# Gated linear attention steps ahead of the selections in a background queue (transformer block, one core)

## The chip, the cores and the metric

One core of a Trainium2 chip runs the whole block as one program. The metric is device time in microseconds (us), the median of several executions. Engines are named as the profile names them: PE (TensorE), DVE (VectorE), ACT (ScalarE), POOL (GpSimd) and SP (SyncE, which issues most transfers).

## What is computed

One layer for a sequence of 1024 positions and width 1024. The part that the change touches is this (cut from the reference):

```python
# attention over the 256 best keys of each query, by an indexer's score
s_idx = einsum('bthd,bsd->bths', q_idx, k_idx)
score = where(causal, einsum('bths,bth->bts', relu(s_idx), w_idx * idx_scale), -inf)
_, sel = lax.top_k(score, 256)
...
# gated linear attention, chunk by chunk
b = cumsum(gc)
A = einsum('bhid,bhjd,bhijd->bhij', qc, kc, exp(b_i - b_j))     # lower triangle
o = einsum('bhij,bhjv->bhiv', A, vc) + einsum('bhid,bhdv->bhiv', qc * exp(b), S)
S = exp(b_last) * S + einsum('bhjd,bhjv->bhdv', kc * exp(b_last - b), vc)
...
x = x + g1 * (concat([rms(att), rms(gla) * silu(go)]) @ w_out)
x = x + g2 * ((silu(gate) * up) @ w_down)
```

## The kernel before

The kernel splits 32-bit operands into a high and a low part and takes three products of them. Its first 160 us or so make the normalised input, the indexer's projections and the scores. The last third and more is the feed-forward part, and ahead of it stands attention (from about 506 us on). Between scores and attention, from 147 to 506 us, stands the stretch of this change: a **main** line of projections on PE, and a **background** of work that is woven into it.

**The main line** is `units(jobs, gq0)`: a list of jobs, each a weight group and a generator. `proj_T_plain` (and `qk_proj`, `qk_park`) yields twice a job, after chains of 24 matmuls of 512 columns (`chain_T`, L241 to L243); below this is a T chain, and such a step says `LONG` = 1.87. `proj_N_plain` yields eight times a job, after chains of 24 matmuls of 256 columns (`chain_N`, L250 to L252); below this is an N chain, a step of 1. `gate_proj` ends with eight steps of `SHORT` = 0.3, without a matmul, which do L911 on DVE. The jobs are, in order: gq0, gk0, gv0, park 2q, gq1, gk1, park 2k, gv1, go0, park 3q, v0, park 3k, v1, go1, and the queries and keys of heads 0 and 1. The weights of the next job are loaded and split when a job begins: the low part is L218 (DVE or POOL).

**The background** is the table `bg`. After each main step, `pump(steps)` goes through it: an entry's `due` grows by its rate times the step's weight, and for each whole unit one step of its generator is issued. The entries are

- `ta` and `td`, the selections. They find the 256th largest score of each row bit by bit, 32 steps each. A step of `ta` is three Sign activations with sums on ACT (L647) and then four little operations on DVE (L649 to L654), each of 128x3 elements. A step of `td` is three compares with sums on DVE (L617) and two little operations (L621, L623). Then each has three steps that call `finish`, which turns a threshold into the mask tile `bias[t]` (L593 to L601);
- `gla0` and `gla1`, the gated linear attention of two pairs of heads (`gla_pair`). For seven levels there are `decays` (POOL L784 and L785, ACT L786), `decayed` (DVE L793, POOL L798), `products` (PE L804) and `masked` (DVE L813), each a step behind the one before. Then come transposes (PE L851, copied by ACT L852), and eight chunks: a DVE operation makes the carried state `diag` (L881, L883), the PE multiplies (L865, L868, L872), the DVE puts the output together (L893);
- `decay`, which prepares the second pair.

The order in `bg` is that of insertion, so `ta` and `td` come first. `pin()` then ties the PE and DVE instructions of the stretch to the order in which they were written: on these two engines the schedule is the program's text. ACT, POOL and SP are ordered by the framework's scheduler. `gs` tiles are a pool of four buffers, `raw` (weights as loaded) of two, `whi` and `wlo` of four.

Of the kernel before, what the change touches and what calls it, by code (L numbers as in the profile page):

```python
# [8 lines left out]
F32 = mybir.dt.float32  # L9
# [8 lines left out]
P = 128  # L18
L = 1024
# [20 lines left out]
WO_POOL = (1, 3, 5, 7)  # L40
H_ACT, H_POOL = (0, 4, 7), (0, 1, 3, 4, 6)

RATE = {"ta": (0.46, 0), "td": (0.46, 1), "gla0": (0.67, 0), "gla1": (0.6, 0), "decay": (0.5, 0),
        "mod2": (1.5, 0), "mods": (1.2, 0), "side": (0.42, 0.6)}

LONG, SHORT = 1.87, 0.3
PRIORITY = {"side": 150, "mods": -40}

PARK_AT = (3, 6, 9, 11)

# [16 lines left out]
def hymba_block_kernel(  # L67
# [44 lines left out]
    def gs(shape, dt=F32):  # L112
        return g(shape, dt, tag="gs", bufs=NGS)
# [234 lines left out]
    bg = {}  # L348

    def pump(steps=1):  # L350

        for name in list(bg):
            it, rate, due = bg[name]
            due += rate * steps
            while due >= 1:
                due -= 1
                with tc.high_priority(PRIORITY[name]) if name in PRIORITY else nullcontext():
                    end = next(it, "end") == "end"
                if end:
                    del bg[name]  # L360
                    break
            else:
                bg[name] = (it, rate, due)

    def drain(name):
# [18 lines left out]
    def gv_proj(p, w):  # L384
        drain("decay")
        gvt[p] = [g([P, 4, 256]) for _ in range(2)]
        if p == 0:
            bg["gla0"] = (gla_pair(0, gqk[0, 0], gqk[0, 1], gvt[0], bTs[0]), *RATE["gla0"])
        yield from proj_N_plain(w, gvt[p])
        if p == 0:  # L390
            bg["decay"] = (gla_decay(1), *RATE["decay"])
        else:
            drain("gla0")
            bg["gla1"] = (gla_pair(1, gqk[1, 0], gqk[1, 1], gvt[1], bTs[1]), *RATE["gla1"])

# [152 lines left out]
    def scores(t):  # L548
        W = (t + 1) * P
        acc = score[t]  # L550
# [34 lines left out]
        return -1.0 if i == 0 else float(1 << (31 - i))  # L585

    def finish(t, thr):
        W = (t + 1) * P
        xs = score[t]
        two = gs([P, 2 * L], BF16)  # L590
        lt, eq = two[:, :W], two[:, L:L + W]
        n2 = small(2, tag="n1")
        V.tensor_scalar(lt, xs, thr, None, ALU.is_lt, ALU.add, accum_out=n2[:, 0:1])  # L593
        V.tensor_scalar(eq, xs, thr, None, ALU.is_equal, ALU.add, accum_out=n2[:, 1:2])
        run = gs([P, L])
        V.tensor_tensor(n2[:, 0:1], n2[:, 0:1], n2[:, 1:2], ALU.add)
        V.tensor_scalar(n2[:, 0:1], n2[:, 0:1], float(TOPK - W), None, ALU.add)
        V.tensor_tensor_scan(run[:, :W], eq, eq, 0.0, ALU.add, ALU.max)
        V.scalar_tensor_tensor(eq, run[:, :W], n2[:, 0:1], eq, ALU.is_gt, ALU.mult)
        V.tensor_tensor(lt, lt, eq, ALU.add)  # L600
        V.tensor_scalar(bias[t], lt, -OFF_BIAS, None, ALU.mult)  # L601

    def topk_dve(ts):
        n = len(ts)
        Z = cst.tile([P, n], I32, name="Zd")
        V.memset(Z, 0)
        for t in ts:
            hi = score[t].bitcast(BF16)[:, 1:2 * (t + 1) * P:2]
            if t in TOP_POOL:
                G.tensor_scalar(top[t], hi, 1.0, 0.0, ALU.mult, ALU.add)  # L610
            else:
                V.tensor_copy(top[t], hi)
        for i in range(32):
            acc = small(8, tag="acc")
            for j, t in enumerate(ts):
                W = (t + 1) * P
                V.tensor_scalar(junk_d[:, :W], top[t] if 0 < i < 16 else score[t],  # L617
                                Z[:, j:j + 1].bitcast(F32), -float(TOPK),
                                ALU.is_ge, ALU.add, accum_out=acc[:, j:j + 1])
            m = small(8, I32, tag="md")  # L620
            V.tensor_scalar(m[:, :n], acc[:, :n], 0.0, flip(i), ALU.is_lt, ALU.mult)  # L621
            if i < 31:
                V.scalar_tensor_tensor(Z, m[:, :n], nextbit(i), Z, ALU.bitwise_xor, ALU.bitwise_xor)  # L623
            else:
                V.tensor_tensor(Z, m[:, :n], Z, ALU.bitwise_xor)
            yield
        bias_tiles((5, 4, 3))
        for j, t in enumerate(ts):
            finish(t, Z[:, j:j + 1].bitcast(F32))
            yield  # L630

    def topk_act(ts):
        n = len(ts)
        Y = cst.tile([P, n], I32, name="Ya")
        F = cst.tile([P, n], I32, name="Fa")
        need = cst.tile([P, n], F32, name="need")
        V.memset(Y.bitcast(F32), 0.0)
        V.tensor_scalar(Y, Y, -2147483648, None, ALU.bitwise_xor)
        V.tensor_copy(F.bitcast(F32), Y.bitcast(F32))
        for j, t in enumerate(ts):  # L640
            V.memset(need[:, j:j + 1], float(2 * TOPK - (t + 1) * P))
        for i in range(32):
            acc = small(8, tag="acca")
            m = small(8, I32, tag="ma")
            for j, t in enumerate(ts):
                W = (t + 1) * P
                A.activation(junk_a[:, :W], score[t], AF.Sign, bias=Y[:, j:j + 1].bitcast(F32),  # L647
                             accum_out=acc[:, j:j + 1])
            V.tensor_tensor(acc[:, :n], acc[:, :n], need, ALU.subtract)  # L649
            V.tensor_scalar(m[:, :n], acc[:, :n].bitcast(I32), 31, -1 if i == 0 else 1 << (31 - i),  # L650
                            ALU.arith_shift_right, ALU.bitwise_and)
            V.copy_predicated(F, m[:, :n], Y)
            if i < 31:
                V.scalar_tensor_tensor(Y, m[:, :n], nextbit(i), Y, ALU.bitwise_xor, ALU.bitwise_xor)  # L654
            else:
                V.tensor_tensor(Y, m[:, :n], Y, ALU.bitwise_xor)
            yield
        bias_tiles((7, 6))
        V.tensor_scalar(Y, Y, -2147483648, None, ALU.bitwise_xor)
        V.tensor_scalar(F, F, -2147483648, None, ALU.bitwise_xor)  # L660
        for j, t in enumerate(ts):
            W = (t + 1) * P
            a1 = small(1, tag="a1")
            V.tensor_scalar(junk_a[:, :W], score[t], F[:, j:j + 1].bitcast(F32), -float(TOPK),
                            ALU.is_ge, ALU.add, accum_out=a1)
            m = small(1, I32, tag="m1")
            V.tensor_scalar(m, a1, 0.0, None, ALU.is_ge)
            V.copy_predicated(Y[:, j:j + 1], m, F[:, j:j + 1])
            finish(t, Y[:, j:j + 1].bitcast(F32))
            yield  # L670


    sh2 = cst.tile([P, KC], F32, name="sh2")
# [93 lines left out]
    def gla_pair(p, gq, gk, gv, bT):  # L767
# [83 lines left out]
            T.transpose(pt[:, cc * P:(cc + 1) * P], gk[:, cc * P:(cc + 1) * P], ident)  # L851
        A.copy(bT, pt)  # L852
        Kn = bT.rearrange("p (a b) -> p a b", b=P)
        yield
        o = gv
        gla_o[p] = o
# [105 lines left out]
    for t in range(4, 8):  # L962
        scores(t)
    bg["ta"] = (topk_act(SEL_A), *RATE["ta"])
    bg["td"] = (topk_dve(SEL_D), *RATE["td"])
    before, mark = {}, [len(nc.cur_bb.bb.instructions)]

# [571 lines left out]
```

## Time and profile before

| | |
|---|---|
| median of 3 runs | 1425.96 us (1423.41 to 1428.74) |
| the profiled execution | 1424.55 us, span 1422.7 us |
| PE busy | 1323.1 us (93%) |
| DVE busy | 913.9 us (64%) |
| ACT busy | 585.5 us (41%) |
| POOL busy | 446.7 us (31%) |
| chain that ended last | PE 63%, DVE 19%, issue 6%, DMA 4%, ACT 4%, POOL 3% |
| granted PE clock, mean | 0.97 |

The shares are means over the whole program. The feed-forward part keeps PE at 10 tenths almost throughout, so the places where PE waits have to be looked for by stretch. A row of a timeline gives the start, the duration, the engine and line, and in brackets the idle time of that engine before it and what ended the idle time.

### The profile page before, as it was taken

The page shows a single profiled execution, that of the slowest core. Times are in us where ns is not written, and L with a number is a line of the kernel's source. Part 1 is how long each engine was busy: PE and PEld are TensorE (multiplying, and loading weights), DVE is VectorE, ACT ScalarE, POOL GpSimd, SP SyncE. Part 2 cuts the span into 40 slices and gives each one's busy share as a digit, 9 for nine tenths or more (in the row PEclk, how much of TensorE's full clock was granted, in tenths as well). Part 3 has the DMA queues.
Part 4 walks back from the last instruction along what each step waited for, and adds up shares of the span by engine and source line. Part 5 has one row for each costly group of instructions (what it writes and reads, how often), then busy time and mean ns, then how long its engine had stood idle before and what let it go on. Part 6 is the DMA issues. An engine that isn't in the chain of part 4 may idle for free.

```text
span 1422.7 us, 18374 instructions
## 1 busy us (share of the span) xinstructions
PE 1323.1 (93%) x6979; PEld 1107.5 (78%) x6979; DVE 913.9 (64%) x1525; ACT 585.5 (41%) x1064; POOL 446.7 (31%) x393
## 2 busy tenths in 40 slices
PE   5899978699899889899997999999999999999997
PEld 4777877498789768788886887778888878888886
DVE  3579889848976935776468656655454556566524
ACT  3377654557464235345574333232233335112202
POOL 3560524413300011223322444334444425232101
PEclk9999989799899999999998999999999999999999
DMA  9600110200220235551221343322212346254102
GB/s 271 201 15 1 32 43 15 60 31 31 90 60 17 71 107 177 208 192 60 86 93 45 104 134 118 104 89 75 88 64 86 108 152 216 94 186 148 45 15 104
DMA packets 93630, 136.35 MB, mean 96 GB/s; under 512 B 6404, under 2 KB 72039, under 8 KB 93543
## 3 DMA queue, kind: packets, MB, share of 16 engines
q1 hardware_dynamic: 89576, 121.49, 26.6%
q0 software_dynamic: 3808, 13.64, 3.0%
q8 instruction: 55, 0.90, 0.3%
q14 instruction: 33, 0.26, 0.1%
q10 hardware_dynamic: 158, 0.06, 0.0%
HBM read 111.04 MB, written 24.13 MB: 95 GB/s over the span
## 4 chain that ended last, share of the span: by engine, by line
PE 63%; DVE 19%; issue 6%; DMA 4%; ACT 4%; POOL 3%; SPq 2%; POOLq 0%; ACTq 0%; DVEq 0%
PE pw L1273 4%; PE pw L1274 4%; PE pw L1275 4%; PE ps L1273 4%; PE ps L1275 4%; PE ps L1274 4%; PE ps L1480 3%; PE ps L1479 3%; PE ps L1481 3%; PE pw L1480 3%; PE pw L1481 2%; PE pw L1479 2%; DVE junk_d L617 2%; DVE h L793 2%; PE ps L250 2%
## 5 line engine op out<-in xcount | busy, mean ns | idle before, releaser
L647 ACT ACTIVATE junk_a<-g,Ya 128x1024 int8<-128x1024 f32 (+2 forms) x96 | 99.9, 1040 | 53.7 <-DVE Ya L654 50.6
L250 PE MATMUL ps<-whi,g 128*128 128x256 f32 x384 | 111.6, 291 | 0.2 <-ACT g L345 0.2
L251 PE MATMUL ps<-whi,g 128*128 128x256 f32 x384 | 109.4, 285 | 0.0
L252 PE MATMUL ps<-wlo,g 128*128 128x256 f32 x384 | 109.3, 285 | 0.0
L1304 POOL TENSOR_TENSOR g<-g,h 128x512 f32<-128x512 f32 x33 | 52.3, 1584 | 139.8 <-issue 53.4
L1445 POOL TENSOR_TENSOR raw<-raw,g 128x1024 f32<-128x1024 f32 x22 | 57.5, 2618 | 111.8 <-DMA raw<-in_w_down_dram 103.3
L243 PE MATMUL ps<-g,wlo 128*128 128x512 f32 x208 | 83.1, 400 | 4.8 <-DVE wlo L218 4.8
L241 PE MATMUL ps<-g,whi 128*128 128x512 f32 x208 | 85.3, 410 | 0.0
L242 PE MATMUL ps<-g,whi 128*128 128x512 f32 x208 | 83.1, 399 | 0.0
L1275 PE MATMUL ps<-g,wlo 128*128 128x512 f32 x192 | 76.0, 396 | 6.3 <-DVE wlo L1266 6.2
L1273 PE MATMUL pw<-g,whi 128*128 128x512 f32 x192 | 76.9, 400 | 1.5 <-DVE h L1322 1.5
L1273 PE MATMUL ps<-g,wlo 128*128 128x512 f32 x192 | 76.0, 396 | 0.7 <-ACT g L1178 0.7
L250 PEld LDWEIGHTS ps<-whi,g 128*128 128x128 f32 x384 | 74.6, 194 | 2.6 <-issue 1.7
L1274 PE MATMUL ps<-g,wlo 128*128 128x512 f32 x192 | 75.7, 394 | 0.4 <-DVE g L1179 0.4
L1274 PE MATMUL pw<-g,whi 128*128 128x512 f32 x192 | 74.9, 390 | 0.0
L1275 PE MATMUL pw<-g,whi 128*128 128x512 f32 x192 | 74.7, 389 | 0.0
L251 PEld LDWEIGHTS ps<-whi,g 128*128 128x128 f32 x384 | 74.5, 194 | 0.0
L252 PEld LDWEIGHTS ps<-wlo,g 128*128 128x128 f32 x384 | 74.4, 194 | 0.0
L617 DVE TENSOR_SCALAR_CACHE_REDUCE junk_d<-g,Zd 128x640 bf16<-128x640 f32 (+5 forms) x96 | 71.4, 743 | 2.3
L1242 POOL TENSOR_TENSOR gs<-raw,raw 128x512 f32<-128x512 f32 x19 | 25.4, 1334 | 119.2 <-DMA raw<-in_w_gate_up_dram 119.2
L1266 DVE TENSOR_TENSOR wlo<-gs,wlo 128x512 fp32r<-128x512 f32 x44 | 39.9, 906 | 29.1 <-ACT wlo L1265 28.6
L1266 DVE TENSOR_TENSOR whi<-gs,whi 128x512 fp32r<-128x512 f32 x44 | 38.7, 879 | 30.9 <-ACT whi L1265 30.4
(408 smaller groups left out, 3881.3 us busy)
## 6 DMA issues: line engine op xcount, KB each, us to landing
raw<-in_w_gate_up_dram SPq DMA_DIRECT2D x42, 512.0 KB, 3.6
g<-in_w_mod_dram SPq DMA_DIRECT2D x24, 512.0 KB, 8.1
raw<-in_w_in_dram SPq DMA_DIRECT2D x24, 512.0 KB, 3.7
whi<-in_w_mod_dram POOLq DMA_DIRECT2D x24, 512.0 KB, 4.8
hid_d<-g SPq DMA_DIRECT2D x22, 512.0 KB, 3.0
raw<-in_w_down_dram SPq DMA_DIRECT2D x22, 512.0 KB, 4.4
gs<-hid_d SPq DMA_DIRECT2D x22, 512.0 KB, 3.5
g<-in_x_dram SPq DMA_DIRECT2D x16, 512.0 KB, 4.5
```

The costliest lines, as they stand in the source:

```text
L241: T.matmul(pt, lhsT=wh, rhs=rh, start=(k == 0), stop=False)
L242: T.matmul(pt, lhsT=wh, rhs=rl, start=False, stop=False)
L243: T.matmul(pt, lhsT=wl, rhs=rh, start=False, stop=(k == KC - 1))
L250: T.matmul(pt, lhsT=rh, rhs=wh, start=(k == 0), stop=False)
L251: T.matmul(pt, lhsT=rl, rhs=wh, start=False, stop=False)
L252: T.matmul(pt, lhsT=rh, rhs=wl, start=False, stop=(k == KC - 1))
L617: V.tensor_scalar(junk_d[:, :W], top[t] if 0 < i < 16 else score[t], Z[:, j:j + 1].bitcast(F32), -float(TOPK), ALU.is_ge, ALU.add, accum_o ...
L647: A.activation(junk_a[:, :W], score[t], AF.Sign, bias=Y[:, j:j + 1].bitcast(F32), accum_out=acc[:, j:j + 1])
L1273: T.matmul(pt, lhsT=w[:, 0, kk, :], rhs=rh, start=(not more and kk == 0), stop=False, skip_group_check=more)
L1274: T.matmul(pt, lhsT=w[:, 0, kk, :], rhs=rl, start=False, stop=False, skip_group_check=more)
L1275: T.matmul(pt, lhsT=w[:, 1, kk, :], rhs=rh, start=False, stop=(kk == 3), skip_group_check=more)
L1480: T.matmul(po[m], lhsT=al[:, r], rhs=wh[:, cc], start=False, stop=False)
```

## The change

Five edits, all in the order and the pace of the background; no instruction is added or dropped.

- `pump` goes through the table with `ta` and `td` last.
- An entry of `CHAINS` (the two gated linear attentions) issues at most one step in a main step; what is due beyond that stays due.
- Rates and starting values: the selections begin with `due` = -1.5 instead of 0 and 1 and run at 0.52 instead of 0.46; the linear attentions run a little faster, and the first begins with 0.9.
- `finish` yields after the two counts, after the scan and at its end, so that a selection's end is three steps a tile; the scan's tile `run` is allocated later.
- `gla_pair` has one more empty step between the transposes' copy and the first chunk.

```diff
-RATE = {"ta": (0.46, 0), "td": (0.46, 1), "gla0": (0.67, 0), "gla1": (0.6, 0), "decay": (0.5, 0),
+RATE = {"ta": (0.52, -1.5), "td": (0.52, -1.5), "gla0": (0.69, 0.9), "gla1": (0.62, 0), "decay": (0.5, 0),
         "mod2": (1.5, 0), "mods": (1.2, 0), "side": (0.42, 0.6)}
...
+CHAINS = ("gla0", "gla1")
...
-        for name in list(bg):
+        for name in sorted(bg, key=lambda name: name in ("ta", "td")):
             it, rate, due = bg[name]
             due += rate * steps
             while due >= 1:
...
                 if end:
                     del bg[name]
                     break
-            else:
+                if name in CHAINS:
+                    break
+            if name in bg:
                 bg[name] = (it, rate, due)
...
         V.tensor_scalar(eq, xs, thr, None, ALU.is_equal, ALU.add, accum_out=n2[:, 1:2])
-        run = gs([P, L])
         V.tensor_tensor(n2[:, 0:1], n2[:, 0:1], n2[:, 1:2], ALU.add)
         V.tensor_scalar(n2[:, 0:1], n2[:, 0:1], float(TOPK - W), None, ALU.add)
+        yield
+        run = gs([P, L])
         V.tensor_tensor_scan(run[:, :W], eq, eq, 0.0, ALU.add, ALU.max)
+        yield
         V.scalar_tensor_tensor(eq, run[:, :W], n2[:, 0:1], eq, ALU.is_gt, ALU.mult)
         V.tensor_tensor(lt, lt, eq, ALU.add)
         V.tensor_scalar(bias[t], lt, -OFF_BIAS, None, ALU.mult)
+        yield
...
-            finish(t, Z[:, j:j + 1].bitcast(F32))
-            yield
+            yield from finish(t, Z[:, j:j + 1].bitcast(F32))
...
         A.copy(bT, pt)
         Kn = bT.rearrange("p (a b) -> p a b", b=P)
         yield
+        yield
```

Three places of the order follow. Rows of the changed kernel have that file's own line numbers, 2 to 7 higher: its L799 is L793, L656 to L661 are L649 to L654, L625 is L617, L872, L875 and L879 are L865, L868 and L872, L918 is L911, L220 is L218.

**DVE, up to the first `decayed`** (L793; in the changed file L799), which feeds the first `products` of the linear attention. Before, four selection steps (L649 to L623) stand ahead of it, of which the last is this, and another follows at once:

```order
L623 SCALAR_TENSOR_TENSOR Zd<-md_1595,Zd 128x3
L649 TENSOR_TENSOR acca_1686<-acca_1686,need 128x3
L650 TENSOR_SCALAR ma_1687<-acca_1686 128x3
L652 COPY_PREDICATED Fa<-ma_1687,Ya 128x3
L654 SCALAR_TENSOR_TENSOR Ya<-ma_1687,Ya 128x3
L617 TENSOR_SCALAR junk_d,acc_1695<-g_800,Zd 128x640
L621 TENSOR_SCALAR md_1699<-acc_1695 128x3
L623 SCALAR_TENSOR_TENSOR Zd<-md_1699,Zd 128x3
L793 TENSOR_TENSOR h_1130<-g_709,gs_1656 64x4x64 x2
L793 TENSOR_TENSOR h_1131<-g_709,gs_1656 64x4x64 x2
L649 TENSOR_TENSOR acca_1763<-acca_1763,need 128x3
```

After, two stand ahead of it, and the second `decayed` follows after one more:

```order
L631 SCALAR_TENSOR_TENSOR Zd<-md_1608,Zd 128x3
L799 TENSOR_TENSOR h_1130<-g_709,gs_1591 64x4x64 x2
L799 TENSOR_TENSOR h_1131<-g_709,gs_1591 64x4x64 x2
L656 TENSOR_TENSOR acca_1672<-acca_1672,need 128x3
L661 SCALAR_TENSOR_TENSOR Ya<-ma_1673,Ya 128x3
L625 TENSOR_SCALAR junk_d,acc_1681<-g_800,Zd 128x640
L631 SCALAR_TENSOR_TENSOR Zd<-md_1685,Zd 128x3
L799 TENSOR_TENSOR h_1132<-g_709,gs_1668 64x4x64 x2
L799 TENSOR_TENSOR h_1133<-g_709,gs_1668 64x4x64 x2
L656 TENSOR_TENSOR acca_1732<-acca_1732,need 128x3
```

(Of each selection step the compares of the two other tiles and some of the little operations are left out here, and in the two places below rows that add nothing.) Two selection steps have moved from ahead of the first `decayed` to behind it.

**PE, the first two chunks of the first linear attention.** Before, both stand behind the same T chain of job park 2k; the second (`pw_2342`) reads the state `diag` that DVE makes from the first (`pw_2335`):

```order
L243 MATMUL ps_2293<-g_155,wlo_2169 128x512
L865 MATMUL pw_2335<-g_1554,g_1624 128x128 x2
L872 MATMUL pw_2335<-g_1554,g_986 64x128 x2
L865 MATMUL pw_2342<-g_1554,g_1624 128x128
L868 MATMUL pw_2342<-diag_2340,g_709 128x128
L872 MATMUL pw_2342<-g_1554,g_986 64x128 x2
L241 MATMUL ps_2355<-g_696,whi_2168 128x512
```

After, the first stands behind that job's second T chain, and an N chain of job gv1 (the L252 to L254 rows, 24 in all) lies between the two:

```order
L245 MATMUL ps_2328<-g_783,wlo_2162 128x512
L872 MATMUL pw_2354<-g_1531,g_1559 128x128 x2
L879 MATMUL pw_2354<-g_1531,g_986 64x128 x2
L252 MATMUL ps_2390<-whi_2275,g_129 128x256
L253 MATMUL ps_2390<-whi_2275,g_130 128x256
L254 MATMUL ps_2390<-wlo_2276,g_129 128x256
L872 MATMUL pw_2418<-g_1531,g_1559 128x128
L875 MATMUL pw_2418<-diag_2416,g_709 128x128
L879 MATMUL pw_2418<-g_1531,g_986 64x128 x2
```

The second chunk has moved behind a T chain and an N chain. On DVE its `diag` now has thirteen selection steps ahead of it, where it had twelve of `ta`, and of `td` twelve too, the first having been done among the scores.

**DVE, the end of the selections.** Before, the last tile's mask is made (L598 to L601), then the sixteen output products of the second gate (L911), then the low part of the weights of head 0's keys (L218, `wlo_4437`):

```order
L598 SCALAR_TENSOR_TENSOR gs_4352<-gs_4348 128x768
L599 SCALAR_TENSOR_TENSOR gs_4348<-gs_4352,n_677_4349,gs_4348 128x768
L600 TENSOR_TENSOR gs_4348<-gs_4348 128x768
L601 TENSOR_SCALAR g_4091<-gs_4348 128x768
L911 SCALAR_TENSOR_TENSOR g_4128<-g_2425,rs_4413,g_4128 128x128 x8
L911 SCALAR_TENSOR_TENSOR g_4129<-g_2426,rs_4413,g_4129 128x128 x8
L218 TENSOR_TENSOR wlo_4437<-raw_4434,whi_4436 128x1024
L404 TENSOR_TENSOR g_4441<-ps_4442,g_4440 128x512
```

After, the same weights (`wlo_4431`) stand ahead of the last step of `finish`, and ten of the sixteen products ahead of its scans:

```order
L918 SCALAR_TENSOR_TENSOR g_4147<-g_2388,rs_4403,g_4147 128x128 x8
L918 SCALAR_TENSOR_TENSOR g_4148<-g_2389,rs_4403,g_4148 128x128 x2
L604 SCALAR_TENSOR_TENSOR gs_4417<-gs_4389 128x768
L604 SCALAR_TENSOR_TENSOR gs_4419<-gs_4395 128x384
L918 SCALAR_TENSOR_TENSOR g_4148<-g_2389,rs_4403,g_4148 128x128 x6
L220 TENSOR_TENSOR wlo_4431<-raw_4428,whi_4430 128x1024
L702 TENSOR_SCALAR h_4619<-whi_4569,cs 128x512
L408 TENSOR_TENSOR g_4435<-ps_4436,g_4434 128x512
L606 SCALAR_TENSOR_TENSOR gs_4389<-gs_4417,n_676_4390,gs_4389 128x768
```

The 32nd step of the selections has moved as well, from behind the last chain of job v1 to behind its second.

## Rows read from the trace of the kernel before

**Rows 1.** The page's first line.

```profile
span 1422.7 us, 18374 instructions
```

**Rows 2.** Windows: stretch, length, busy of PE, PEld, DVE, ACT, POOL, PEclk, DMA.

```profile
159.00:205.00 46.00, 36.25 (x257) 34.51 (x256) 35.21 (x92) 29.48 (x55) 17.21 (x15) 0.89 0.05 12
205.00:273.00 68.00, 48.77 (x245) 40.22 (x243) 66.12 (x117) 36.26 (x54) 29.03 (x19) 0.87 0.16 47
273.00:315.00 42.00, 41.51 (x270) 35.53 (x270) 19.84 (x72) 22.34 (x63) 4.79 (x2) 0.93 0.12 38
338.00:385.00 47.00, 37.16 (x234) 34.27 (x233) 44.67 (x87) 23.31 (x36) 21.30 (x14) 0.89 0.26 79
```

**Rows 3.** Timeline of PE: the first matmul after each long wait.

```profile
184.94 0.55 PE L804 MATMUL pw<-h,gs 128*128 128x128 f32 x1 [9.35 <-DVE h L793]
...
227.32 0.55 PE L804 MATMUL pw<-h,gs 128*128 128x128 f32 x1 [5.51 <-DVE h L793]
...
265.95 0.48 PE L872 MATMUL pw<-g,g 128*64 128x128 f32 x2 [7.88 <-ACT g L852]
...
273.49 0.55 PE L868 MATMUL pw<-diag,g 64*128 64x128 f32 x1 [6.12 <-DVE diag L881]
...
358.77 0.55 PE L804 MATMUL pw<-h,gs 128*128 128x128 f32 x1 [5.50 <-DVE h L793]
...
377.03 0.35 PE L804 MATMUL pw<-h,gs 128*128 128x128 f32 x1 [3.41 <-DVE h L793]
...
494.73 0.79 PE L243 MATMUL ps<-g,wlo 128*128 128x512 f32 x1 [4.84 <-DVE wlo L218]
...
512.83 0.69 PE L999 MATMUL pw<-g,g 128*128 128x384 f32 x1 [5.32 <-DVE mx L1004]
```

**Rows 4.** Timeline of DVE: the first selection steps, and the first state `diag`.

```profile
163.70 0.50 DVE L649 TENSOR_TENSOR acca<-acca,need 128x3 f32<-128x3 f32 x1 [4.69 <-ACT junk_a L647]
...
171.66 0.16 DVE L649 TENSOR_TENSOR acca<-acca,need 128x3 f32<-128x3 f32 x1 [1.00 <-ACT junk_a L647]
...
174.90 0.16 DVE L623 SCALAR_TENSOR_TENSOR Zd<-md,Zd 128x3 int32<-128x3 int32 x1
...
273.06 0.28 DVE L881 COPY diag<-pw 128x128 f32<-128x128 f32 x1
```

**Rows 5.** Groups of DVE from 159 to 273 us: busy, mean ns, idle before.

```profile
L654 DVE SCALAR_TENSOR_TENSOR Ya<-ma,Ya 128x3 int32<-128x3 int32 x12 | 9.0, 750 | 0.4
...
L649 DVE TENSOR_TENSOR acca<-acca,need 128x3 f32<-128x3 f32 x12 | 6.4, 533 | 9.0 <-ACT junk_a L647 8.9
```

**Rows 6.** Timeline of DVE at the end of the scores.

```profile
151.80 1.02 DVE L638 TENSOR_SCALAR Ya<-Ya 128x3 int32<-128x3 int32 x1
```

**Rows 7.** Timeline of POOL, then of DVE, at one place.

```profile
231.15 3.39 POOL L836 TENSOR_TENSOR gs<-g,g 128x1024 f32<-128x1024 f32 x1 [4.70 <-PE pw L804]
...
232.19 2.36 DVE L649 TENSOR_TENSOR acca<-acca,need 128x3 f32<-128x3 f32 x1
```

**Rows 8.** Timeline of PE: first matmuls after chunk 7, of job go1, of head 0's queries.

```profile
315.07 0.38 PE L250 MATMUL ps<-whi,g 128*128 128x256 f32 x1
...
455.23 0.38 PE L250 MATMUL ps<-whi,g 128*128 128x256 f32 x1
...
478.36 0.40 PE L241 MATMUL ps<-g,whi 128*128 128x512 f32 x1
```

**Rows 9.** Groups of DVE from 455 to 506 us: busy, mean ns, idle before.

```profile
L593 DVE TENSOR_SCALAR_CACHE_REDUCE gs<-g,Ya 128x1024 bf16<-128x1024 f32 (+2 forms) x3 | 3.4, 1146 | 0.1
```

**Rows 10.** Timelines of DVE, ACT and again DVE at the end.

```profile
489.26 4.28 DVE L911 SCALAR_TENSOR_TENSOR g<-g,rs,g 128x128 f32<-128x128 f32 x16
493.46 1.21 DVE L218 TENSOR_TENSOR wlo<-raw,whi 128x1024 fp32r<-128x1024 f32 x1
...
499.57 1.05 ACT L217 CAST whi<-raw 128x1024 fp32r<-128x1024 f32 x1 [14.95 <-DMA raw<-in_w_in_dram]
...
511.02 1.54 DVE L698 SCALAR_TENSOR_TENSOR h<-whi,cs,h 128x512 f32<-128x512 f32 x2 [4.88 <-DMA whi<-in_w_mod_dram]
```

More of the change, by code (lines that the diff above doesn't have):

```diff
@@ L668, in topk_act @@
             V.copy_predicated(Y[:, j:j + 1], m, F[:, j:j + 1])
-            finish(t, Y[:, j:j + 1].bitcast(F32))
-            yield
+            yield from finish(t, Y[:, j:j + 1].bitcast(F32))
     sh2 = cst.tile([P, KC], F32, name="sh2")
```

## The prediction

> **What bounds the kernel now.** I read the page first: span 1422.7 us [rows 1], PE busy for 93% of it. A change that only reorders can win at most what PE waits, so I next looked for its waits. The timeline of PE from 147 to 506 us holds eight of over 3 us [rows 3]. Four lie in the first linear attention: 9.35, 5.51, 7.88, 6.12 = 28.9 us. Two lie in the second: 5.50 + 3.41 = 8.9. Two lie at the end: 4.84 + 5.32 = 10.2. Together 47.9 us.
>
> Then the windows [rows 2]: who is full while PE waits? From 205 to 273 us DVE is busy for 66.12 of 68, PE for 48.77. From 273 to 315 it turns round: PE 41.51 of 42, DVE 19.84. From 338 to 385 DVE is full again, 44.67 of 47. So in these stretches the time is that of DVE's program, and PE's order matters only where it needs DVE's results.
>
> What fills DVE is in its timeline [rows 4]. From the little operations at 171.66 to the last at 174.90 (+0.16), a selection step, one of `ta` with one of `td`, takes 3.4 us, of which the little four of `ta` are 0.7. At 273.06 stands the first `diag`, for which PE waits last: DVE gets there 114 us after the scores' last operation (163.70 less 4.69 idle = 159.0). Of these 114 us DVE waits 9.0 for ACT's counts [rows 5], so 105 are work.
>
> Not all of that is its own work. The groups [rows 5] give the four little operations away: L654 takes 750 ns and L649 533 on the mean, but 0.16 alone [rows 4]. These two alone lose 15.4 - 24 x 0.16 = 11.6 us. Where it goes is seen at one place [rows 7]: L649 starts at 232.19 while POOL's L836 runs, lasts 2.36 instead of 0.16, and ends with it (234.55 and 234.54). DVE stood still for POOL.
>
> **The change, part by part.** The same instructions run, so I price only places.
>
> *First linear attention.* Three things move DVE's first `diag`.
>
> 1. The start. td's first step (2.7 us: 3.4 less 0.7) now comes after the scores; two `wlo` of about 1.2 (as one in [rows 10]) and two little operations of 1.02 [rows 6] stand ahead of the scores' products instead of among them. That is 2.7 + 2.4 + 2.0 = 7.1 us off the scores' end: DVE is done at 152, not 159.0. The bounds: 156, if PE's scores set their end, and 152.
> 2. The work. One more selection step (thirteen of each for twelve, `td`'s first among them): +3.4. Two casts of weights that now stand ahead of `diag`, for which ACT's L217 with 1.05 [rows 10] is the nearest row, `td`'s preparation of a single copy in it: +2.0 (bounds 0 and 3). So 105 + 5.4 = 110.4 us.
> 3. The idle time before L649, 9.0: as the linear attention now fills in, I take 6; bounds 0 and 9.
>
> 152 + 110.4 + 6 gives the first `diag` at 268.5 instead of 273.06. That alone is 4.6 us. The larger part is on PE: the second chunk, which reads `diag`, now stands behind one more T chain and one more N chain. From the start of the eight N chains at 455.23 to 478.36 [rows 8] one takes 2.89. From 478.36 to 489.9 (494.73 less its wait of 4.84) PE ran 50 matmuls of 512 columns, 0.23 each, so a T chain of 24 is 5.5 (at the 0.40 of the first's record, 9.6: the bound). PE, which waited 28.9 us, has time for these 8.4 us in its waits, so after `diag` it has 8.4 us less to do. Before, from 273.49 [rows 3] to the step after chunk 7 at 315.07 [rows 8] are 41.58, nearly all of it PE's work; that becomes 33.2, which ends at about 302. **-13 us.** Check from the other side: PE without a wait would have reached the old place at 273.49 - 28.9 = 244.6 and reaches the new one at 253; it waits 268.5 - 253 = 15.5 instead of 28.9, which is 13.4 less. DVE has room behind: 19.84 busy of 42.
>
> *Second linear attention.* `products` of the last level stands one N chain sooner, one selection step more stands ahead, and the rest has the same density. DVE is full here, so its work sets the time: **0**, with bounds of -8.9 (both waits go) and +3.4 (the selection step).
>
> *`finish` among the last chunks.* The counts of the first two tiles now stand between two chunks: two counts of 1.15 [rows 9] and two shorter ones, at most 4 x 1.15 = 4.6 us, beside a T chain of 5.5 on PE. I take 0; if the cover is gone, up to +4.6.
>
> *The end.* PE waits 4.84 us at 494.73 [rows 3] for `wlo` (L218), which DVE makes at 493.46, behind all three tiles' `finish` and L911 [rows 10]. Now `wlo` stands ahead of the last step of `finish`, and the selections' last step ends six steps sooner. L911 still needs the gate's last activations on ACT, after PE's N chains end at 478.36 [rows 8], so `wlo` comes at about 486, before PE wants it at 489.9 (494.73 - 4.84). **-4.8.** Behind it hangs a second chain: with `wlo` done, the buffer of `raw` is free, the next weights are loaded, ACT casts them (L217, 14.95 idle for that DMA), DVE's L698 waits for a DMA of its own, 4.88 [rows 10], and then come PE's scores of attention, with a wait of 5.32 for `mx` [rows 3]. That chain starts 7.4 us sooner (493.46 to 486), PE 4.84 sooner, so 2.6 of the 5.32 go. **-2.6.** Bounds of the two: 0 and -10.2.
>
> *DMA.* One store of queries passes one load of weights on SP's queue, two jobs before anyone reads them: 0. (DMA share in these windows: 0.05 to 0.26 [rows 2].)
>
> Sum: -13 + 0 + 0 - 4.8 - 2.6 = -20.4. The profiled execution took 1424.55 us, 1.4 below the median of 1425.96; I count from it: **1404 us**. The granted clock is 0.87 to 0.89 where PE waits [rows 2], and after the wait at 494.73 a matmul takes 0.79 at the 1.2 GHz level, where 0.40 is shown at 478.36 [rows 8]. Fewer waits may lift that; I don't count it, and let it speak for the low end.
>
> **The rivals.** What a measurement can tell from no change is about 0.5%, 7.1 us.
>
> *A. PE takes over as the bound.* If DVE, better mixed, loses none of the 11.6 us to POOL, `diag` comes at 257, only 4 after PE. The first part then gives -25 or, with ACT's idle time gone too, all 28.9; with the end's -7.4 that is 1388 to 1392. For it: the loss is a matter of meeting, not of work. Against: POOL's instructions keep their order and follow the same chains. 0.15.
>
> *B. The end doesn't move.* The last transfers may hang on something that I didn't see, and `finish` may be late all the same. Only the first part counts: 1411.5. For it: the wait before L217 is a DMA's. Against: the wait at 494.73 is DVE's, plainly. 0.14.
>
> *C. It comes back.* What PE gains in front it waits for later, since DVE's total stays: 1424. Against: the 22 us that DVE is free from 273 to 315. 0.10.
>
> *D. POOL takes the gain: slower.* POOL is busy for 17.21 + 29.03 = 46.2 us from 159 to 273 [rows 2], and DVE has lost at least 11.6 to it [rows 5, 7]. The change puts `decayed` and the masks, which follow POOL's results, ahead of the selections' little operations, so other instructions with two inputs stand beside POOL's. If all of the 46.2 were lost, that would be 34.6 more, far above the gain. It decides from 20 us more over both linear attentions (13 + 7.4). Say two thirds of POOL's time is lost: in the first 31 of 46.2, so 19 more; in the second, with POOL busy for 21.30 of 47 [rows 2] and a quarter of it lost now as in the first, 14 less 5, so 9 more. -13 + 19 + 9 - 7.4 = +7.6: 1432. For it: [rows 7]. Against: the compares of L617 are most of a selection step and keep their time. 0.09.
>
> The Trainium skill has a rule for D: on its page "SBUF — State Buffer", section "Who interferes with whom", DVE with two SBUF inputs and a GpSimd instruction that reads SBUF lock each other out for a whole instruction, and whichever starts second stands still. By that rule an order with more such pairs side by side is slower, and this one could be; the blocked L649 agrees with it.
>
> **How the numbers follow.** The forecast has 0.52. Its own range: the errors of the first part (4: `diag` at 264 to 272), the second (6, half of its bounds) and the end (5, half), taken as independent, make 9: 1394 to 1414. The 8 in 10: I leave out C and D (0.19) and take in A, B and the clock: 1382, which is A's 1388 and 6 less for the second part, to 1421, B's with the 4.6 of `finish` and the 3.4 + 1.5 of a selection step with a loss. Faster by over 0.5%: forecast, A, B = 0.81. Within: C, 0.10. Slower: D, 0.09.
>
> **What would show it.** Right: the first `diag` on DVE at 265 to 272, PE's waits before it 13 to 18 us in all; the first N chain after chunk 7 at 299 to 306; the second part's waits near 9; the wait for `wlo` gone, that for `mx` under 4. A: PE's waits before `diag` under 5. B: L911 or a DMA still ahead of PE's first chain of head 0's keys. D: L649 and L654 at over 1.2 us on the mean, or `decayed` far longer. I am wrong if `diag` comes after 273, or if PE's waits are as long, 45 us or more, at other places.

## The result, and the profile after

The changed kernel took **1409.49 us** (median of 4 runs, 1407.03 to 1414.02) against 1424.68 of the kernel before (4 runs): a ratio of 0.9894, 95% interval 0.9857 to 0.9931, faster by 1.1%. The forecast was 1404, range 1382 to 1421. The profiled execution has a span of 1406.1 us, 16.6 less than before. The sign came out as forecast and the size at three quarters (15.2 us between the medians, where 20.4 were forecast). The shares of the places did not: the front gave little, and the end gave more than its part.

The timeline of PE, the first matmul after each long wait, answers to [rows 3]:

```profile
179.65 0.64 PE L810 MATMUL pw<-h,gs 128*128 128x128 f32 x3 [1.92 <-DVE h L799]
...
203.58 0.35 PE L810 MATMUL pw<-h,gs 128*128 128x128 f32 x1 [1.50 <-DVE h L799]
...
250.14 0.80 PE L245 MATMUL ps<-g,wlo 128*128 128x512 f32 x1 [5.29 <-DVE wlo L220]
...
279.35 0.55 PE L875 MATMUL pw<-diag,g 64*128 64x128 f32 x1 [6.74 <-DVE diag L888]
...
345.54 0.35 PE L810 MATMUL pw<-h,gs 128*128 128x128 f32 x1 [2.94 <-DVE h L799]
...
357.78 0.55 PE L810 MATMUL pw<-h,gs 128*128 128x128 f32 x1 [2.45 <-DVE h L799]
...
373.62 0.35 PE L810 MATMUL pw<-h,gs 128*128 128x128 f32 x1 [2.19 <-DVE h L799]
...
502.00 0.44 PE L1006 MATMUL pw<-g,g 128*128 128x384 f32 x1 [2.25 <-DVE mx L1011]
```

The longest waits of the first linear attention fell from 28.9 to 15.5 us in four rows each. That this is the number of the prediction's check is chance, since shorter waits (1.44 and 1.29 the longest of them) come on top: from the first T chain of gk0 to that chunk all of PE's waits add up to 29.5 us before and 20.4 after. And the first N chain after chunk 7 came at 312.85 instead of 315.07: only 2.2 us sooner. The next table sets the starts of equal PE work side by side, from the timelines of both:

| start on PE | before | after | difference |
|---|---|---|---|
| first T chain of gk0 | 146.80 | 152.29 | +5.5 |
| first N chain after chunk 7 | 315.07 | 312.85 | -2.2 |
| head 0's queries | 478.36 | 477.09 | -1.3 |
| second T chain of head 0's keys | 501.19 | 493.44 | -7.8 |
| span | 1422.7 | 1406.1 | -16.6 |

So PE waited 9.0 us less ahead of `diag`, about what the two added chains take there, but it had lost 5.5 us before the stretch began, and DVE's first `diag` came at 278.92, 5.9 later than before. The windows [rows 2] say the same: PE busier by 5 and 9 us, and in the window from 273 us on, where it had been full, six less.

```profile
159.00:205.00 46.00, 41.66 (x292) 38.91 (x290) 36.59 (x85) 28.53 (x52) 23.17 (x20) 0.96 0.05 12
205.00:273.00 68.00, 58.24 (x286) 48.19 (x286) 62.37 (x127) 38.62 (x60) 26.19 (x17) 0.92 0.16 46
273.00:315.00 42.00, 35.65 (x240) 30.92 (x241) 21.92 (x80) 23.58 (x69) 5.74 (x4) 0.88 0.13 39
338.00:385.00 47.00, 38.07 (x234) 34.86 (x233) 45.76 (x91) 24.99 (x38) 20.47 (x14) 0.89 0.25 79
```

Two places show what made the front late. ACT, at the start of the scores, now has the cast of a weight (L219, park 2q) between the first and the second Relu (L562). It waits for its DMA, and PE with it (2.93 us at 120.95):

```profile
115.27 0.71 ACT L562 ACTIVATE gs<-pw 128x640 f32<-128x640 f32 x1
119.25 1.04 ACT L219 CAST whi<-raw 128x1024 fp32r<-128x1024 f32 x1 [3.27 <-DMA raw<-in_w_in_dram]
120.20 1.29 ACT L562 ACTIVATE gs<-pw 128x640 f32<-128x640 f32 x2
```

At the end of the scores, ACT does three exponentials of the linear attention ahead of the selections' first counts (L654), and waits for POOL before them; DVE stands idle for those counts:

```profile
160.00 1.06 ACT L792 ACTIVATE gs<-gs 128x1024 f32<-128x1024 f32 x1 [2.95 <-POOL gs L791]
162.12 1.06 ACT L792 ACTIVATE gs<-gs 128x1024 f32<-128x1024 f32 x1 [1.06 <-POOL gs L791]
163.09 0.56 ACT L337 COPY g<-ps 128x512 f32<-128x512 f32 x1
163.55 1.15 ACT L654 ACTIVATE junk_a<-g,Ya 128x1024 int8<-128x1024 f32 x1
```

```profile
159.06 1.06 DVE L568 TENSOR_TENSOR g<-g,dmin 128x128 f32<-128x128 f32 x1
167.86 0.16 DVE L656 TENSOR_TENSOR acca<-acca,need 128x3 f32<-128x3 f32 x1 [7.74 <-ACT junk_a L654]
...
278.92 0.28 DVE L888 COPY diag<-pw 128x128 f32<-128x128 f32 x1
```

At the end the wait for `wlo` is gone: DVE makes it at 483.39 instead of 493.46 [rows 10], and `mx` comes earlier by as much, behind the same DMA wait of 4.9 us.

```profile
478.79 0.61 DVE L918 SCALAR_TENSOR_TENSOR g<-g,rs,g 128x128 f32<-128x128 f32 x2 [2.89 <-ACT g L911]
...
483.39 1.22 DVE L220 TENSOR_TENSOR wlo<-raw,whi 128x1024 fp32r<-128x1024 f32 x1
...
500.20 1.54 DVE L704 SCALAR_TENSOR_TENSOR h<-whi,cs,h 128x512 f32<-128x512 f32 x2 [4.94 <-DMA whi<-in_w_mod_dram]
```

And PE's clock stays up. Windows of the kernel before, after its two waits, and then of the changed one at the same work (the column before the DMA share is the granted clock: 1.00 is the 2.4 GHz level throughout, and a mean below it holds some time at the 1.2 GHz level):

```profile
494.70:501.30 6.60, 6.57 (x23) 5.33 (x24) 1.88 (x4) 1.53 (x2) 0.00 (x0) 0.78 0.54 157
513.00:530.00 17.00, 17.00 (x72) 13.81 (x73) 4.37 (x14) 4.92 (x15) 2.23 (x4) 0.85 0.30 93
```

```profile
488.00:494.00 6.00, 6.00 (x28) 4.99 (x27) 4.91 (x9) 1.90 (x3) 0.74 (x1) 1.00 0.44 132
502.00:517.00 15.00, 14.85 (x70) 12.03 (x71) 4.54 (x14) 4.92 (x15) 2.20 (x4) 1.00 0.34 106
```

### The profile page after: what moved, and what is told of

Its sections match the earlier page's. It is cut to its first block, busy times and chain, and to the rows that moved or that the text cites. A ratio compares the mean times of both kernels' runs of the same rounds, so it can differ in the third digit from the quotient of the medians.

```text
span 1406.1 us, 18387 instructions
## 1 busy us (share of the span) xinstructions
PE 1319.4 (94%) x6979; PEld 1104.1 (79%) x6979; DVE 915.8 (65%) x1525; ACT 586.4 (42%) x1064; POOL 445.8 (32%) x393
## 4 chain that ended last, share of the span: by engine, by line
PE 68%; DVE 16%; issue 5%; DMA 3%; ACT 3%; SPq 2%; POOL 2%; DVEq 0%; ACTq 0%; POOLq 0%
PE pw L1280 5%; PE pw L1281 4%; PE pw L1282 4%; PE ps L1280 4%; PE ps L1282 4%; PE ps L1281 4%; PE pw L1486 3%; PE pw L1487 3%; PE ps L1486 3%; PE ps L1487 3%; PE pw L1488 3%; PE ps L1488 3%; DVE junk_d L625 3%; PE ps L252 2%; PE ps L253 2%
## 5 line engine op out<-in xcount | busy, mean ns | idle before, releaser
L654 ACT ACTIVATE junk_a<-g,Ya 128x1024 int8<-128x1024 f32 (+2 forms) x96 | 99.9, 1041 | 50.5 <-DVE Ya L661 47.8
L252 PE MATMUL ps<-whi,g 128*128 128x256 f32 x384 | 113.1, 295 | 3.3 <-DVE whi L217 1.4
L254 PE MATMUL ps<-wlo,g 128*128 128x256 f32 x384 | 110.5, 288 | 0.7 <-DVE wlo L220 0.7
L252 PEld LDWEIGHTS ps<-whi,g 128*128 128x128 f32 x384 | 75.6, 197 | 6.4 <-issue 3.5
L254 PEld LDWEIGHTS ps<-wlo,g 128*128 128x128 f32 x384 | 75.6, 197 | 0.9 <-DVE wlo L220 0.9
L625 DVE TENSOR_SCALAR_CACHE_REDUCE junk_d<-g,Zd 128x640 bf16<-128x640 f32 (+5 forms) x96 | 71.4, 744 | 2.4
```

Of the source, the lines that this page charges most:

```text
L252: T.matmul(pt, lhsT=rh, rhs=wh, start=(k == 0), stop=False)
L254: T.matmul(pt, lhsT=rh, rhs=wl, start=False, stop=(k == KC - 1))
```

## The experiments

Each run's ratio is to runs of the kernel before on the same chip. All edits are on the changed kernel, except where the kernel before is named.

**1. The end alone.** The old front, with `finish` in three steps and the selections at 0.52.

```diff
-RATE = {"ta": (0.52, -1.5), "td": (0.52, -1.5), "gla0": (0.69, 0.9), "gla1": (0.62, 0), "decay": (0.5, 0),
+RATE = {"ta": (0.52, 0), "td": (0.52, 1), "gla0": (0.67, 0), "gla1": (0.6, 0), "decay": (0.5, 0),
-CHAINS = ("gla0", "gla1")
+CHAINS = ()
-        for name in sorted(bg, key=lambda name: name in ("ta", "td")):
+        for name in list(bg):
...
         yield
-        yield
         o = gv
```

> The old front (selections first in the table, two steps of a linear attention allowed, td's first step among the scores) with finish in three steps and the selections at 0.52. Theory 1 (the end's gain comes from the selections being over sooner, whatever the front does): PE's wait for wlo (4.84) and most of that for mx (5.32) go, the low clock behind them too; 10 to 13 us below the kernel before, so 1412 to 1415. Theory 2 (the end is early only because the new front lets everything come sooner): within 4 us of the kernel before, 1421 to 1428, with the wait for wlo still there.

Measured: 1416.39 us, ratio 0.9943 (0.9923 to 0.9963). PE's timeline has no wait over 1.2 us between the second linear attention and the `mx` of attention, and that one is short. But the first `products` wait longer than in either kernel:

```profile
190.20 0.55 PE L810 MATMUL pw<-h,gs 128*128 128x128 f32 x1 [13.82 <-DVE h L799]
...
276.92 0.55 PE L875 MATMUL pw<-diag,g 64*128 64x128 f32 x1 [6.12 <-DVE diag L888]
...
508.61 0.44 PE L1006 MATMUL pw<-g,g 128*128 128x384 f32 x1 [1.21 <-DVE mx L1011]
```

Head 0's queries start at 484.74, 6.4 later than before; the T chain at 523.73 before starts at 517.53, 6.2 sooner. So the end gains 12.6 us with the old front too (theory 1), and the higher rate in the old order costs 6.4 ahead of it. The forecast of that run had left this out, and the time lies 1.4 above its range. The new front takes these 6.4 back and 1.3 more.

**2. `finish` in one step again.**

```diff
-        yield
         run = gs([P, L])
         V.tensor_tensor_scan(run[:, :W], eq, eq, 0.0, ALU.add, ALU.max)
-        yield
```

> The changed kernel with finish in one step again. Theory 1 (the rate ends the selections early; the split only keeps finish from standing in the way of the chunks): no wait for wlo at 490 us, but bursts of 10 us and more on DVE between two chunks of the second linear attention, PE waits 8 to 15 us there: 1418 to 1425. Theory 2 (the split is what frees the end): the wait for wlo is back at its place, none at the chunks: 1416 to 1420.

Measured: 1420.27 us, 0.9974 (0.9962 to 0.9986). No wait for `wlo`; two new waits between chunks of the second linear attention, behind 14.6 us of the selections' end on DVE, most of it `finish` (from 427.00 to the `diag` at 441.55), and another 13:

```profile
441.94 0.58 PE L875 MATMUL pw<-diag,g 64*128 64x128 f32 x1 [5.29 <-DVE diag L890]
...
455.49 0.37 PE L875 MATMUL pw<-diag,g 64*128 64x128 f32 x1 [3.53 <-DVE diag L890]
```

Theory 1: the rate frees the end, and the split is what makes that rate affordable. Without the split some 11 of the 15 us are gone.

**3. ACT's cast behind the scores.** `relu[0]` is the last Relu of the scores; only ACT's order changes by hand.

```diff
-        hi, lo = wsplit(raw, [P, 8, 128], lo_eng, ring, hi_eng=hi_eng)
+        with tc.issue_after(relu[0].ins) if c0 == C_Q + 2 * P else nullcontext(): hi, lo = wsplit(raw, [P, 8, 128], lo_eng, ring, hi_eng=hi_eng)
```

> The changed kernel, with ACT's cast of the weights of park 2q behind the last Relu of the scores instead of behind the first, where it waited 3.27 us for its DMA. Theory 1 (this wait is why the scores end at 160.1 instead of 152 to 156 on DVE): scores' last operation on DVE at 156 to 157, PE's T chain at 152.3 now at 147 to 148, first diag 3 to 4 us sooner, 1405 to 1407. Theory 2 (the next thing is late: ACT's exponentials wait for POOL ahead of the first counts): scores end sooner, but diag at 277 or later, 1408 to 1411.

Measured: 1407.81 us, 0.9894 (0.9866 to 0.9922): not told apart from the changed kernel. In the trace the scores do end sooner, 154.31 + 1.05 instead of 160.12, and the T chain of 152.29 starts at 147.97. The first counts come 4.9 sooner (162.96 for 167.86). The idle time before them stays:

```profile
154.31 1.05 DVE L568 TENSOR_TENSOR g<-g,dmin 128x128 f32<-128x128 f32 x1
162.96 0.16 DVE L656 TENSOR_TENSOR acca<-acca,need 128x3 f32<-128x3 f32 x1 [7.60 <-ACT junk_a L654]
```

PE's wait for the first `diag` ends at 277.33, 2.0 sooner. So the cast explains most of the late scores, but the gain is mostly lost again ahead of `diag`: nearer to theory 2. The other 2.9 us go into the selections' little operations (the six groups of experiment 4): up to `diag` these take 33.3 us here and 30.4 in the changed kernel, 78 operations in both.

**4. The masks in PSUM.** PSUM is the memory to which PE writes the kernel's `ps` and `pw` tiles; SBUF holds the other tiles that these operations use. `held` is a slice of one PSUM tile. The masks `ma` and `md` and the constant `need` move there, so that no little operation of a selection has two inputs in SBUF. The order on PE, POOL and SP is unchanged; that on ACT, which the scheduler makes, differs in 22 of 1072 instructions.

```diff
+    held = lambda a, b, t=[]: (t or t.append(ps()) or t)[0][:, a:b]
...
-            m = small(8, I32, tag="md")
+            m = held(0, 8).bitcast(I32)
-        need = cst.tile([P, n], F32, name="need")
+        need = held(16, 16 + n)
-            m = small(8, I32, tag="ma")
+            m = held(8, 16).bitcast(I32)
```

> The changed kernel with the masks ma and md and the constant need in PSUM, so that the selections' little operations have one SBUF input each; order on PE, POOL and SP unchanged. Theory 1 (DVE loses time to POOL because both its inputs are in SBUF): mean of L661, L631 and L656 from 159 to 273 us under 0.3 instead of 0.5 to 0.7, DVE at its first diag 10 to 15 us sooner, or ACT's counts become its wait; 1396 to 1403. Theory 2 (the long little operations are long for another reason, or PSUM costs as much): means as they are, 1407 to 1412.

Measured: **1396.53 us**, 0.9805 (0.9785 to 0.9826), clearly below the changed kernel. Groups of DVE from 159 to 273 us, first of the changed kernel and then of this one (busy, mean ns, idle before):

```profile
L631 DVE SCALAR_TENSOR_TENSOR Zd<-md,Zd 128x3 int32<-128x3 int32 x12 | 7.1, 593 | 0.4
L661 DVE SCALAR_TENSOR_TENSOR Ya<-ma,Ya 128x3 int32<-128x3 int32 x12 | 5.9, 490 | 0.4
L659 DVE COPY_PREDICATED Fa<-ma,Ya 128x3 int32<-128x3 int32 x12 | 5.6, 471 | 0.4
L656 DVE TENSOR_TENSOR acca<-acca,need 128x3 f32<-128x3 f32 x12 | 4.8, 398 | 10.9 <-ACT junk_a L654 10.8
...
L657 DVE TENSOR_SCALAR ma<-acca 128x3 int32<-128x3 int32 x12 | 3.3, 274 | 0.5
...
L629 DVE TENSOR_SCALAR md<-acc 128x3 int32<-128x3 f32 x12 | 2.7, 226 | 0.4
```

```profile
L657 DVE TENSOR_SCALAR ps<-acca 128x3 int32<-128x3 int32 x14 | 2.3, 165 | 0.5
L659 DVE COPY_PREDICATED Fa<-ps,Ya 128x3 int32<-128x3 int32 x14 | 2.3, 164 | 0.5
L661 DVE SCALAR_TENSOR_TENSOR Ya<-ps,Ya 128x3 int32<-128x3 int32 x14 | 2.2, 160 | 0.5
L629 DVE TENSOR_SCALAR ps<-acc 128x3 int32<-128x3 f32 x13 | 2.1, 165 | 0.5
L656 DVE TENSOR_TENSOR acca<-acca,ps 128x3 f32<-128x3 f32 x14 | 2.1, 151 | 12.7 <-ACT junk_a L654 12.6
L631 DVE SCALAR_TENSOR_TENSOR Zd<-ps,Zd 128x3 int32<-128x3 int32 x13 | 2.1, 162 | 0.4
```

The six cost 29.4 us in twelve steps of the changed kernel; at 0.161, the mean of the six below, these 72 are 11.6: 17.8 us were spent standing. DVE's first `diag` comes at 267.01 instead of 278.92; 1.9 of this stands already at the scores' end, which the edit does not touch. Theory 1. That it is POOL for which they stand is seen without the edit too: in the kernel before, 29 of these operations take over 300 ns, and each of the 29 ends within 0.15 us of the end of a POOL instruction. Not all of the 17.8 reaches `diag`: from the first counts to there DVE's work is 10.9 us less, as other operations got longer, the six that make `wlo` from 7.3 to 10.1 us and the eight scans from 3.2 to 5.3.

The Trainium skill names both kinds of pair, on its page "SBUF — State Buffer", section "Who interferes with whom": two SBUF inputs on DVE against a reading GpSimd instruction, and a `tensor_scalar` in a mode that uses both ports. The runs agree: the four with two inputs and the two TENSOR_SCALAR all fall to the same 0.15 to 0.17 once one side lies in PSUM. In which mode the latter ran, no run shows.

**5. The masks in PSUM, on the kernel before.** The same four lines.

> The kernel before with the masks and the constant of the selections in PSUM (the same edit as in the run on the changed kernel). Theory 1 (the loss to POOL bounds DVE's program in either order, and the change does not touch it): 10 to 14 us below the kernel before, 1411 to 1415, PE's four waits in the first linear attention 10 us shorter in all; the change's own gain stays the same on top. Theory 2 (the new order made the loss, so that the edit repairs something of the change): 0 to -5, 1420 to 1425.

Measured: 1402.41 us, 0.9842 (0.9814 to 0.9869): 22 us less, more than either theory had. From 159 us to its `diag` the six groups take 11.6 us in twelve steps; in the kernel before they take 33.9 from 159 to 273 ([rows 5] has the two largest), so 22.3 had been lost to POOL. PE still waits at the end:

```profile
472.72 0.80 PE L243 MATMUL ps<-g,wlo 128*128 128x512 f32 x1 [4.84 <-DVE wlo L218]
```

Neither theory as it stood: the loss was there before the change (theory 1), and the change had made it smaller up to `diag`, from 22.3 to 17.8. To the end of the selections, with the second linear attention, it is 32.5 before and 32.0 after. With the masks in PSUM the change as a whole is worth 5.9 us (1402.41 to 1396.53, with intervals that just overlap) instead of 15.

**6 to 8. The front's parts, each undone alone:** the starting values, the limit, the place in the table.

```diff
-RATE = {"ta": (0.52, -1.5), "td": (0.52, -1.5), "gla0": (0.69, 0.9), "gla1": (0.62, 0), "decay": (0.5, 0),
+RATE = {"ta": (0.52, 0), "td": (0.52, 1), "gla0": (0.69, 0.9), "gla1": (0.62, 0), "decay": (0.5, 0),
```

```diff
-CHAINS = ("gla0", "gla1")
+CHAINS = ()
```

```diff
-        for name in sorted(bg, key=lambda name: name in ("ta", "td")):
+        for name in list(bg):
```

> The changed kernel with the selections' starting values at 0 and 1 again (td's first step among the scores; 14 and 15 steps ahead of the first diag instead of 13 and 13, four ahead of the first products instead of two). Theory 1 (DVE's program up to diag sets the time): about one and a half steps of 3.4 us more ahead of diag, less 3 us of td's first step that the scores hide: +2 to +6, 1411 to 1416. Theory 2 (the late start costs as much in the scores as it gives): -2 to +1, 1407 to 1411.

> The changed kernel without the limit of one step of a linear attention in a main step: the first diag has 11 selection steps ahead of it instead of 13, and PE does one T chain and one N chain less ahead of it. Theory 1 (both count: 2 x 3.4 = 6.8 us less of DVE against 8.4 us less of PE's projections in PE's waits): +1.6, within 1407 to 1413. Theory 2 (the limit is what gives the gain, as PE's projections hide the wait): +5 to +9, 1414 to 1419.

> The changed kernel with the selections first in the table again: order on PE the same, on DVE each decayed one selection step later, the first diag behind 13 steps as before. Theory 1 (only what stands ahead of diag counts; a longer wait at the first products comes back as a shorter one at diag): 1408 to 1412. Theory 2 (each wait of the products counts): 3 to 5 us more in the first linear attention and in the second, 1413 to 1419.

Measured: 1408.66 (0.9896, 0.9874 to 0.9917), 1410.80 (0.9909, 0.9889 to 0.9929), 1411.40 (0.9913, 0.9894 to 0.9932). None is told apart from the changed kernel. PE's longest waits of the first linear attention, in that order of the three kernels:

```profile
185.03 0.55 PE L810 MATMUL pw<-h,gs 128*128 128x128 f32 x1 [12.21 <-DVE h L799]
...
278.05 0.55 PE L875 MATMUL pw<-diag,g 64*128 64x128 f32 x1 [7.30 <-DVE diag L888]
```

```profile
268.53 0.55 PE L875 MATMUL pw<-diag,g 64*128 64x128 f32 x1 [10.61 <-DVE diag L888]
```

```profile
182.96 0.55 PE L810 MATMUL pw<-h,gs 128*128 128x128 f32 x1 [6.34 <-DVE h L799]
```

The waits move, and the first N chain after chunk 7 comes at 311.69, 310.09 and 312.53, against 312.85. So for the limit and the place in the table theory 1 holds: a wait ahead of `diag` only moves, and a `diag` that is sooner by what PE then has less ahead of it gives nothing. The limit's run is the plainest: `diag` 10.8 us sooner, the end of the chunks 2.8. For the starting values theory 2 holds, and the traces show what the late start costs in the scores. With the starting values of before, PE's T chain of 152.29 starts at 146.86, and DVE waits 4.69 us for the first counts. With the late start it waits 7.74, also where the selections stand first in the table (the second row):

```profile
163.81 0.50 DVE L656 TENSOR_TENSOR acca<-acca,need 128x3 f32<-128x3 f32 x1 [4.69 <-ACT junk_a L654]
```

```profile
166.77 0.16 DVE L656 TENSOR_TENSOR acca<-acca,need 128x3 f32<-128x3 f32 x1 [7.74 <-ACT junk_a L654]
```

So both places that made the front late, ACT's cast and its exponentials ahead of the counts, come from the late start and not from the order in the table. A smaller loss to POOL helps the run with the old starting values, 11.9 us up to `diag` for 17.8.

**9 to 11. Versions with the masks in PSUM:** the end alone on the old front (experiments 1 and 4), the starting values of before (6 and 4), and, as the last, ACT's cast behind the scores (3 and 4) with `td` ahead of `ta`:

```diff
-        for name in sorted(bg, key=lambda name: name in ("ta", "td")):
+        for name in sorted(bg, key=lambda name: ("td", "ta").index(name) + 1 if name in ("ta", "td") else 0):
```

> The old front with the selections at 0.52 and finish in three steps (as in the run on the end alone), and the masks in PSUM. Theory 1 (the new front only saves what DVE loses to POOL; without that loss the old front is at least as good, and the end's gain adds to it): 22 us of the edit on the kernel before plus 9 of the end, 1390 to 1394, below the changed kernel with the same edit. Theory 2 (the new front is better by itself): the old front costs 6 us as it did without the edit, 1398 to 1404.

> The changed kernel with the starting values of before and the masks in PSUM. Theory 1 (as td's first step is again hidden among the scores and ACT's cast no longer stands between two Relu, DVE is at diag sooner): 3 to 6 us below the changed kernel with the masks in PSUM, 1390 to 1394. Theory 2 (one more selection step ahead of diag takes it back, as it did with the masks in SBUF): 1395 to 1399.

> The changed kernel with the masks in PSUM, ACT's cast behind the scores, and td ahead of ta in the table, so that td's first step fills what DVE waits for ACT's first counts (7.4 us). Theory 1: the cast's 4 us and td's first step 2.7 us both come off the time to diag: 1389 to 1393. Theory 2 (ACT, whose counts wait for its exponentials and these for POOL, is the bound once DVE isn't): 1394 to 1398.

Measured: 1395.33 (0.9803, 0.9788 to 0.9817), 1399.79 (0.9838, 0.9819 to 0.9857) and **1390.92** (0.9767, 0.9749 to 0.9785). The first: with the masks in PSUM the old front and the new (1396.53) are not told apart, where without that they were 7 us apart (1416.39 and 1409.49, with intervals that just overlap). So the new front is worth something only while DVE loses time to POOL. How is not shown: to the end of the selections the six groups lose 34.0 us in experiment 1 and 32.0 in the changed kernel, which is 2 of the 7. The number lies between the two theories' ranges, and the old front is not better either. The second: nearer to theory 2, 3 us worse than the late start of experiment 4, with intervals that just overlap. The third beats both kernels: 31.8 us below the kernel before on its chip (1422.68), 18.6 below 1409.49. Its first counts are waited for less, 5.41 instead of 7.40 in experiment 4, as theory 1 has it; what the cast and what `td` give apart was not tried.

```profile
163.58 0.16 DVE L656 TENSOR_TENSOR acca<-acca,ps 128x3 f32<-128x3 f32 x1 [5.41 <-ACT junk_a L654]
```

## Why the prediction was right, and where not

The time fell into the range, but by the prediction's own sign (wrong if `diag` comes after 273) its account of the front is wrong: `diag` came at 278.92. The sum came out by luck, as the parts below show.

*What bounds.* Right in the main: in the first linear attention the time is that of DVE's program up to `diag`. Experiment 4, which makes DVE's operations shorter, moves `diag` by 11.9 us and the kernel by 13. But experiment 7, where `diag` came 10.8 sooner and the kernel was no faster, shows that PE's work ahead of `diag` counts with it.

*The first term, -13, failed: -2.2.* By its steps:

- PE's side held. The 8.4 us of chains ahead of `diag` came off the rest: 312.85 less 279.35 is 33.5, where 33.2 was forecast.
- "DVE is done at 152" failed: 160.1, 8 us late. The step counted DVE's own operations and had 156 as the other end, with PE as the cause. What happened was on ACT, whose order moves too: a cast that waits for its DMA. In experiment 3, without it, the scores end at 155.4, so the cast is 4.8 of the 8, and the rest is near the bound of 156.
- "I take 6" for DVE's idle time failed: 12.05 (7.74, and 3.02 and 1.29 later). The growth is in the first, 4.69 before: with the late start (experiments 6 and 8) ACT has its exponentials ahead of the counts, and these wait for POOL.
- "110.4 us" of work was 3.6 too much: 278.92 - 160.12 - 12.05 = 106.75, as less was lost to POOL (17.8 for 22.3).

Together 8.1 + 6.05 - 3.65 = 10.5, and `diag` was 10.4 late.

*The second term, 0:* to head 0's queries it became -1.3 from -2.2, so +0.9. The pieces of `finish` among the chunks were indeed hidden; experiment 2 shows the price that the split avoids.

*The end, -7.4, was too small:* from 478.36 to the T chain at 523.73 it is -11.5. The wait for `wlo` went (4.84), that for `mx` fell from 5.32 to 2.25 (3.07, forecast 2.6). The rest of 3.6 is the term that the forecast named and did not count: the clock behind the waits, granted 0.78 and 0.85 before and 1.00 after. From the start of the first T chain of head 0's keys to the next were 501.19 - 489.27 = 11.92 before and 5.44 after, 6.48 less, of which the wait is 4.84: 1.64 are the clock's. From the end of the wait for `mx` to the T chain at 523.73 were 10.9 before and 8.9 after, the same matmuls without a wait: another 2.0. Behind attention's start another 3.8 came, for which the forecast has no term and no run was made. Set side by side, the same matmuls show where: 1.7 by 615 us, among attention's own waits; 1.2 from 774.95 to 777.50, behind a wait of 6.2 in both kernels, where the same matmuls took 2.55 us at a granted clock of 0.50 before and 1.37 at 1.00 after; and 0.8 after 1120.

So -2.2 + 0.9 - 11.5 - 3.8 = -16.6: the range held it because the end and what lies behind made up for part of the missing front. Rival A (no loss to POOL) did not come, as 17.8 us were still lost. Rival B (the end doesn't move) was the wrong way round. Rival C (what is gained in front doesn't last) is nearest to the front's sum, but not in its way: the gain was missing ahead of `diag`, not lost behind it. Rival D's mechanism is real and large, 22.3 us before, but its sign was wrong: the new order loses less to POOL up to `diag` and about as much in all. The prediction had bounded it by two of the six groups, 11.6.

## What to carry to other kernels

When a stretch is bound by one engine's program, add up everything that this program waits for, ACT's order too: a change of two engines' order moves casts and exponentials on a third, and each can then wait ahead of what is needed, here for a DMA and for POOL. Look in the groups for small operations whose mean is several times their shortest: here they lost 22 of DVE's 114 us, and moving a few columns of their operands to PSUM gave the kernel before more than the whole reordering did. Count a wait that ends together with the slow clock behind it.

## What was not expected of the hardware

A TENSOR_SCALAR with a single SBUF input (L650, 128x3) also stood for POOL: 410 ns on the mean from 159 to 273 us in the kernel before, 165 with its output in PSUM. And an operation of 128x3 elements costs no more with one operand in PSUM: 151 to 165 ns, against 0.16 to 0.17 us alone with all in SBUF.
